# Grouped-query scores in pairs of heads, with the keys' low parts multiplied on 64 rows of TensorE

## The chip, the cores and the metric

The kernel runs on one core of a Trainium2 chip. The metric is the device time of one execution in microseconds (us). Three runs of the kernel before gave 1169.85, 1170.03 and 1171.18; the median is 1170.03.

## What is computed

Two layers of an encoder over 512 positions of width 1024, all in float32. Each layer projects the input into three groups of heads, mixes positions in each, projects back, adds and normalises, and then runs a gated FFN of width 2816. The change concerns the second group, grouped-query attention: 8 query heads of dimension 64 share 2 key/value heads.

```python
def gqa_attention(q, k, v):          # q: (b, s, 2, 4, 64), k and v: (b, s, 2, 64)
    scale = B_HEAD_DIM ** -0.5

    def block(qb):                   # 128 queries at a time
        s = jnp.einsum('bqhgd,bkhd->bhgqk', qb, k).astype(jnp.float32) * scale
        p = jax.nn.softmax(s, axis=-1).astype(v.dtype)
        return jnp.einsum('bhgqk,bkhd->bqhgd', p, v)

    return sweep_query_blocks(block, q)
```

## The kernel before

**Precision.** A float32 operand is kept as two parts of a faster matmul type, a high part (a rounded copy) and a low part (what the rounding left). A product is then high by high, high by low and low by high, three matmuls into one PSUM bank (`mm`, L240). Conversions are a copy on ACT and a subtraction on DVE or POOL (`put`, L248).

**Scores of the second group.** A head has only 64 dimensions, so the 128 rows of TensorE hold two parts at once. `qTB` (L176) has a slice of 128 rows by 512 queries for each of the 8 heads: for head (j, c), with j the key/value head and c = 0 to 3, the 64 rows of half j (`own`) hold the query's high part, the 64 rows of the other half its low part (L730 to L734). `kT` (L170) has two slices for each j: the key's high part on both halves (slice 2j), and its low part on both halves (slice 2j + 1; the second half is a copy by POOL, L717). One head is then two matmuls of 128 rows by 512 columns, first by slice 2j, then by slice 2j + 1 (L863, L864); they give all four products of parts.

**Softmax.** In `attn_b` (L837), for each block `qb` of 128 queries, each j and each c: the two score matmuls into one of three banks in turn (5, 6, 7; `score_banks`), the maximum (DVE, L866), its product with the head's scale (DVE, L869), the exponential with its sum (ACT, L873), the reciprocal (DVE, L875) and the normalisation (DVE, L876) into one of four slots of `E`. The head is put on a list (`pend`); as soon as three are on it, the oldest is finished (L841): four transposes on TensorE (L91) into one of two banks, and a copy to `W[j]` by ACT (L848). After the last head of a block, `pv_b` (L885) multiplies the probabilities with the values: 8 float32 matmuls whose results are 64 columns wide, j = 1 and j = 0 in turn on the two halves of TensorE's columns (the trace has two records for each).

**Order.** Each part of a layer is a generator; `Flow.run` (L105) advances the one of lowest rank whose time has come, by a planner's clock that each matmul advances by the cost written in its call (0.216 for the two score matmuls). A scheduler then moves the instructions of each engine by the priorities in `PRI` (L51) and by its own estimate of when operands are ready. While `attn_b` waits for softmax, `main` (L1089) fills TensorE with the query projection, then with `w_out` (L897): first the rows of the first and third group (`mixAC`), later those of this group (`mixB`), always three matmuls at a time. Each engine runs its instructions strictly in the order that comes out.

Of the kernel before, what the change touches and what calls it, by code (L numbers as in the profile page):

```python
# [14 lines left out]
AF = mybir.ActivationFunctionType  # L15
ALU = mybir.AluOpType
AX = mybir.AxisListType
PSUM = bass.MemoryType.PSUM

P = 128  # L20
# [9 lines left out]
LAT = {"c out": 1.6, "c": 1.05, "rope_a": 2.23, "split": 3.7, "turned": 0.61, "mix": 1.69, "rope_k": 4.08, "rope_q": 16.38, "split_k": 45.7, "soft_a": 2.05, "soft_b": 2.99, "copy": 1.27, "norm_a": 4.33, "put": 0.72, "ln": 4.93}  # L30
RATE = {"rank0": 3.09, "rank1": 2.96, "rank2": 0.16, "rank3": 4.47, "rank4": 4.88, "rank5": 32.35, "rankpv": 2.01, "rankev": 0, "rankx": 0, "a": 2.42, "a1": 2.34, "b": 0.12}
KNOBS = {"pin": 0, "pool1": 2, "pool2": 0, "pool3": 0, "poolac": 0, "poolbb": 1, "da": 2, "db": 3, "t2": 1, "rsb": 1, "ntail": 6, "qm": 1, "sb": 1, "cb": 0, "actdiv": 0, "kdup": 1, "splitq": 0, "splitk": 0, "ropet": 1, "aorder": 0}
# [14 lines left out]
def r(ap):  # L47
    return ap.bitcast(F32R)
# [223 lines left out]
def build(nc, tc, d, ctx_pools):  # L272
    pool, psum = ctx_pools
    k = Trunk(nc, tc, d, pool, psum)
    NS = 2
    X, xT, B, st, ident = k.X, k.xT, k.banks, k.st, k.ident
    ACT, DVE, POOL, SYNC = nc.scalar, nc.vector, nc.gpsimd, nc.sync
    F = PE = k.flow
# [4 lines left out]
    def small(n):  # L283

        if stp[0] + n > st.shape[1]:
            stp[0] = KEEP
        a = st[:, stp[0]:stp[0] + n]
        stp[0] += n
        return a
# [153 lines left out]
    def load_gb(l, which):  # L443
        SYNC.dma_start(out=k.GB[:, 0:D], in_=d[f"ln{which}_g"][l:l + 1, :].broadcast_to([P, D]))
        SYNC.dma_start(out=k.GB[:, D:2 * D], in_=d[f"ln{which}_b"][l:l + 1, :].broadcast_to([P, D]))
# [23 lines left out]
    def transposes(out, src):  # L469
        for c in range(4):  # L470
            PE.transpose(out[:, c * P:(c + 1) * P], src(c), ident)
# [6 lines left out]
    turn_banks, score_banks, prob_banks = (itertools.cycle(B[i] for i in b) for b in (tb_, ((5, 6, 7), (5, 6, 7, 2))[0], (3, 4)))  # L478

    def layer(l):  # L480
# [219 lines left out]
        def turn_b():  # L700
            yield ev("c mixed")
            kb = B[2]
            for tb in range(NT):
                yield ev("rope k", tb)
                PE.transpose(kb[:, tb * P:(tb + 1) * P], k.t1[tb % 2][:, 0:P], ident)
                busy.discard(tb % 2)

            with pri("kev"):
                for j in range(2):
                    own = slice(64 * j, 64 * j + 64)  # L710
                    other = slice(64 * (1 - j), 64 * (1 - j) + 64)
                    for u in (own, other):
                        ACT.copy(out=r(k.kT[u, 2 * j]), in_=kb[own])
                        if u is own or not KNOBS["kdup"]:
                            DVE.tensor_tensor(out=r(k.kT[u, 2 * j + 1]), in0=kb[own], in1=k.kT[own, 2 * j], op=ALU.subtract)
                    if KNOBS["kdup"] == 1:
                        POOL.tensor_copy(out=r(k.kT[other, 2 * j + 1]), in_=k.kT[own, 2 * j + 1])  # L717
                    elif KNOBS["kdup"] == 2:
                        ACT.copy(out=r(k.kT[other, 2 * j + 1]), in_=k.kT[own, 2 * j + 1])
            F.mark(ev("k"), 1.0)  # L720
            yield ev("scores a", 0)
            k.start_q_b(l)
            for tb in range(NT):
                yield ev("rope q", tb)
                with pri("qev"):
                    tbk = next(turn_banks)
                    transposes(tbk, lambda c: k.t1[tb % 2][:, c * P:(c + 1) * P])
                    busy.discard(tb % 2)
                    tv = tbk.rearrange("p (c t) -> p c t", c=4)
                    qv = k.qTB.rearrange("p (c j) t -> p c j t", j=2)[:, :, :, tb * P:(tb + 1) * P]  # L730
                    for j in range(2):
                        own, other = slice(64 * j, 64 * j + 64), slice(64 * (1 - j), 64 * (1 - j) + 64)
                        ACT.copy(out=r(qv[own, :, j]), in_=tv[own])
                        DVE.tensor_tensor(out=r(qv[other, :, j]), in0=tv[own], in1=qv[own, :, j], op=ALU.subtract)  # L734
                F.mark(ev("q", tb), LAT["turned"])
            k.start_mix_b(l)
            load_gb(l, 1)
            F.mark(ev("mix b"))


        def attn_a():
# [5 lines left out]
            for hp in range(2):  # L747
# [3 lines left out]
                for qb in range(NT):  # L751
                    for hh in range(2):
                        e = [E[:, (2 * (i % 2) + m) * T:(2 * (i % 2) + m + 1) * T] for m in range(2)]
                        i += 1
                        with pri("soft_a"):
                            ss = [s0v[:, qb, hh:hh + 1], small(1)]
                            for m in range(2):
                                S = next(score_banks)
                                PE.matmul(S, r(qk[0][:, 2 * hh + m, qb * P:(qb + 1) * P]), r(qk[1][:, 2 * hh + m]), 0.216, start=True, stop=True)
                                nm = small(1)  # L760
                                DVE.tensor_reduce(out=nm, in_=S, op=ALU.max, axis=AX.X, negate=True)
                                ACT.activation(out=e[m], in_=S, func=AF.Exp, bias=nm, accum_out=ss[m])
                            r1 = small(1)
# [73 lines left out]
        def attn_b():  # L837
            yield ev("pv a", 1)
            pend = []

            def finish(job):  # L841
                qb, j, c, p_, t = job
                yield max(0.0, t - F.now)
                with pri("turn_pb"):
                    tbk = next(prob_banks)
                    transposes(tbk, lambda c_: p_[:, c_ * P:(c_ + 1) * P])
                    wT = W[j].rearrange("p k (c q) -> p k c q", c=4)
                    ACT.copy(out=wT[:, :, c], in_=tbk.rearrange("p (k q) -> p k q", k=NT))  # L848
                if j == 1 and c == 3:
                    if qb == 0:  # L850
                        yield ev("mix b")
                    F.add(pv_b(qb), RATE['rankpv'])
                    yield ev("pv b", qb)

            n = 0
            for qb in range(NT):
                yield ev("q", qb)
                for j in range(2):
                    for c in range(4):
                        t_s = F.now  # L860
                        with pri("soft_b"):
                            S = next(score_banks)
                            for i in range(2):  # L863
                                PE.matmul(S, r(k.qTB[:, 2 * c + j, qb * P:(qb + 1) * P]), r(k.kT[:, 2 * j + i]), 0.216, start=i == 0, stop=i == 1)  # L864
                            nm = small(1)
                            DVE.tensor_reduce(out=nm, in_=S, op=ALU.max, axis=AX.X, negate=True)  # L866
                            sc = rsq[:, qb, 2 * c + j:2 * c + j + 1]
                            nb = small(1)
                            DVE.tensor_scalar_mul(out=nb, in0=nm, scalar1=sc)  # L869
                            p_ = E[:, (n % 4) * T:(n % 4 + 1) * T]  # L870
                            n += 1
                            s_ = small(1)
                            ACT.activation(out=p_, in_=S, func=AF.Exp, bias=nb, scale=sc, accum_out=s_)  # L873
                            rs = small(1)
                            DVE.reciprocal(out=rs, in_=s_)  # L875
                            DVE.tensor_scalar_mul(out=p_, in0=p_, scalar1=rs)  # L876
                        pend.append((qb, j, c, p_, F.now + LAT["soft_b"]))
                        yield RATE["b"] / 2
                        if len(pend) >= KNOBS['db']:
                            yield from finish(pend.pop(0))  # L880
                        yield max(0.0, t_s + RATE["b"] - F.now)
            for job in pend:
                yield from finish(job)

        def pv_b(qb):  # L885
            yield LAT["turned"]
            with pri("pv_b"):
                pv = B[2]
                for kb in range(NT):
                    for j in (1, 0):  # L890
                        PE.matmul(pv[64 * j:64 * j + 64, :], k.V[:, kb, 256 + j * 64:256 + (j + 1) * 64], W[j][:, kb], 0.44,
                                  start=kb == 0, stop=kb == NT - 1)
                k.put([m[:, :, qb * P:(qb + 1) * P] for m in k.mixB], pv.rearrange("p (c q) -> p c q", c=4))
            F.mark(ev("pv b", qb))
            F.mark(ev("mix b", qb), LAT["put"])
# [292 lines left out]
```

## Time and profile before

| | |
|---|---|
| median of three runs | 1170.03 us |
| the profiled execution's own time | 1170.78 us |
| its span | 1169.0 us |
| TensorE (PE) busy | 1145.8 us |
| DVE, ACT, POOL busy | 840.9, 624.9, 128.8 us |
| granted clock of TensorE | 0.996 of full speed over the span |

The span runs from the first to the last instruction; the execution's own time has 1.78 us around it. The busy time of TensorE counts a matmul until its modelled end, and matmuls are pipelined (one starts every 0.23 us, each lasts 0.40), so a share of 98% says that it hardly ever waits, not that it is at its peak. The second group's softmax stands twice in the span: from 123 to about 215 us in the first layer, and from 706 to about 798 us in the second.

### The profile page before, as it was taken

To read this page: it belongs to the slowest core of one execution; us is meant where nothing else is said; L and a number is where in the kernel's file an instruction comes from. 1 tells how busy PE (TensorE), PEld (TensorE's weight loads), DVE (VectorE), ACT (ScalarE), POOL (GpSimd) and SP (SyncE) were. 2 spreads that over 40 slices of the span, in tenths; PEclk is the share of its full clock that TensorE was granted. 3 is DMA by queue.
4 is the path that set the end of the run, shared out by engine and by line. 5 is a ranking of instruction groups with operands and counts; after the bars stand their busy time and mean duration, and the time that the engine had idled before them with its cause. 6 is when DMAs were issued, how large, how long until landed. Compare 5 with 4: busy or idle time off the path is not lost.

```text
span 1169.0 us, 18110 instructions
## 1 busy us (share of the span) xinstructions
PE 1145.8 (98%) x6930; PEld 977.8 (84%) x6930; DVE 840.9 (72%) x1532; ACT 624.9 (53%) x1348; POOL 128.8 (11%) x118
## 2 busy tenths in 40 slices
PE   9999899999999999999989998999999999999997
PEld 7787676799999999888768776767999999998886
DVE  5778977886888887333764889778777888873346
ACT  5778866454555555322254788654545655552220
POOL 1233230100000000000231342301000000000001
PEclk9999999999999999999999999999999999999999
DMA  8402140253242312334051021303432424132321
GB/s 286 151 1 91 37 127 1 91 163 108 73 135 83 115 68 81 100 91 126 25 152 62 2 89 45 119 1 107 146 108 73 145 73 133 49 91 90 96 85 73
DMA packets 32775, 107.86 MB, mean 92 GB/s; under 512 B 4657, under 2 KB 5681, under 8 KB 32689
## 3 DMA queue, kind: packets, MB, share of 16 engines
q1 hardware_dynamic: 32688, 106.71, 28.7%
q8 instruction: 54, 0.88, 0.3%
q14 instruction: 33, 0.26, 0.1%
HBM read 104.60 MB, written 2.10 MB: 91 GB/s over the span
## 4 chain that ended last, share of the span: by engine, by line
PE 87%; DVE 4%; DMA 3%; issue 3%; ACT 2%; POOL 2%; SPq 0%; POOLq 0%; ACTq 0%; DVEq 0%
PE bank L87 81%; PE bank L91 5%; DMA RAW<-w_in 2%; POOL st L292 1%; DVE XT L252 1%; ACT va L819 1%; DMA we<-w_in 1%; DVE st L866 0%; POOL rope L603 0%; POOL RING L266 0%; ACT RING L251 0%; DVE qTB L734 0%; DVE va L827 0%; DVE earlyr L252 0%; DVE RING L252 0%
## 5 line engine op out<-in xcount | busy, mean ns | idle before, releaser
L87 PE MATMUL bank<-XT,RING 128*128 128x256 f32 (+1 forms) x2304 | 305.6, 293 | 0.0
L87 PEld LDWEIGHTS bank<-XT,RING 128*128 128x128 f32 x2304 | 293.3, 191 | 7.7
L87 PE MATMUL bank<-RING,XT 128*128 128x512 f32 x576 | 160.8, 409 | 2.7 <-DVE RING L266 2.0
L292 POOL TENSOR_TENSOR st<-st 128x1 f32<-128x1 f32 (+2 forms) x44 | 54.1, 1229 | 929.1 <-DVE st L431 799.7
L251 ACT CAST RING<-ffnwe 128x512 fp32r<-128x512 f32 x156 | 96.0, 620 | 103.3 <-PE bank L87 61.5
L251 ACT CAST RING<-RAW 128x1024 fp32r<-128x1024 f32 (+1 forms) x114 | 97.0, 854 | 80.3 <-PE bank L87 33.4
L252 DVE TENSOR_TENSOR RING<-ffnwe,RING 128x512 fp32r<-128x512 f32 x156 | 107.1, 689 | 42.7 <-ACT RING L251 23.5
L87 PEld LDWEIGHTS bank<-RING,XT 128*128 128x128 f32 x576 | 106.7, 192 | 26.4 <-DVE RING L266 2.6
L252 DVE TENSOR_TENSOR RING<-RAW,RING 128x1024 fp32r<-128x1024 f32 (+1 forms) x106 | 101.8, 962 | 34.8 <-ACT RING L251 27.6
L87 PE MATMUL bank<-blkr,RING 128*128 128x256 f32 x864 | 105.5, 282 | 0.0
L87 PEld LDWEIGHTS bank<-blkr,RING 128*128 128x128 f32 x864 | 103.8, 189 | 0.0
L87 PE MATMUL bank<-RING 128*128 128x512 f32 x384 | 88.5, 390 | 0.0
L87 PEld LDWEIGHTS bank<-RING 128*128 128x128 f32 x384 | 72.0, 188 | 15.1
L91 PE MATMUL bank<-ident,we 128*128 128x128 f32 x400 | 62.0, 274 | 5.7 <-DVE va L827 5.5
L91 PEld LDWEIGHTS bank<-ident,we 128*128 128x128 f32 x400 | 47.9, 140 | 22.4 <-ACT rope L662 4.4
L873 ACT ACTIVATE we<-bank,st 128x512 f32<-128x512 f32 x64 | 50.5, 790 | 8.1 <-DVE st L869 7.7
L344 DVE TENSOR_TENSOR ffnwe<-ffnwe 128x512 f32<-128x512 f32 x80 | 54.6, 685 | 0.3
L87 PE MATMUL bank<-blkq,RING 128*128 128x256 f32 x432 | 54.3, 282 | 0.0
L87 PE MATMUL bank<-XT,mixAC 128*128 128x512 f32 x192 | 52.3, 404 | 0.6 <-DVE XT L252 0.5
L87 PEld LDWEIGHTS bank<-blkq,RING 128*128 128x128 f32 x432 | 52.6, 189 | 0.0
L848 ACT COPY we<-bank 128x512 f32<-128x512 f32 x64 | 37.8, 592 | 25.6 <-PE bank L91 25.6
L866 DVE TENSOR_REDUCE st<-bank 128x1 f32<-128x512 f32 x64 | 43.7, 686 | 10.7 <-PE bank L87 10.4
(210 smaller groups left out, 1925.9 us busy)
## 6 DMA issues: line engine op xcount, KB each, us to landing
RAW<-w_dn SPq DMA_DIRECT2D x44, 512.0 KB, 3.6
ffnwe<-w_gu SPq DMA_DIRECT2D x40, 512.0 KB, 4.5
RAW<-w_gu SPq DMA_DIRECT2D x32, 512.0 KB, 3.6
RAW<-w_in SPq DMA_DIRECT2D x28, 512.0 KB, 3.7
RAW<-w_out SPq DMA_DIRECT2D x16, 512.0 KB, 3.7
ffnw<-w_gu SPq DMA_DIRECT2D x16, 512.0 KB, 4.9
we<-xT SPq DMA_DIRECT2D x8, 256.0 KB, 5.4
X<-x SPq DMA_DIRECT2D x4, 512.0 KB, 5.4
```

The costliest lines, as they stand in the source:

```text
L87: self.pin(self.nc.tensor.matmul(out, lhs, rhs, **kw))
L91: self.pin(self.nc.tensor.transpose(out, src, ident))
L251: nc.scalar.copy(out=r(dst[0]), in_=src)
L252: (low or nc.vector).tensor_tensor(out=r(dst[1]), in0=src, in1=dst[0], op=ALU.subtract)
L292: POOL.tensor_tensor(out=out, in0=src, in1=k.mhalf[:, 0:n], op=ALU.pow)
L344: tc.keep_in_program_order(DVE.tensor_tensor(out=out, in0=x, in1=y, op=ALU.subtract))
L819: ACT.activation(out=oT[:, h * 64:(h + 1) * 64], in_=tbk[:, h * 64:(h + 1) * 64], func=AF.Square, accum_out=ms[:, h:h + 1])
L848: ACT.copy(out=wT[:, :, c], in_=tbk.rearrange("p (k q) -> p k q", k=NT))
L866: DVE.tensor_reduce(out=nm, in_=S, op=ALU.max, axis=AX.X, negate=True)
L873: ACT.activation(out=p_, in_=S, func=AF.Exp, bias=nb, scale=sc, accum_out=s_)
```

## The change

Two heads, (0, c) and (1, c), are taken together, with a bank each. For each, the first matmul stays as it was (128 rows by the key's high part, so high by high and low by high). The second now covers only the 64 rows of half j: the query's high part by the key's low part; low by low is dropped. The planner is told 0.108 for it, in place of 0.216. The two second matmuls stand on different halves of the rows. The copy of the low part to the other half of the rows (L717) is no longer made. Softmax of both heads follows, both go on the list, and as long as three or more are on it the oldest is finished.

```diff
                     for u in (own, other):
                         ACT.copy(out=r(k.kT[u, 2 * j]), in_=kb[own])
-                        if u is own or not KNOBS["kdup"]:
-                            DVE.tensor_tensor(out=r(k.kT[u, 2 * j + 1]), in0=kb[own], in1=k.kT[own, 2 * j], op=ALU.subtract)
-                    if KNOBS["kdup"] == 1:
-                        POOL.tensor_copy(out=r(k.kT[other, 2 * j + 1]), in_=k.kT[own, 2 * j + 1])
...
+                    DVE.tensor_tensor(out=r(k.kT[own, 2 * j + 1]), in0=kb[own], in1=k.kT[own, 2 * j], op=ALU.subtract)
...
             for qb in range(NT):
                 yield ev("q", qb)
-                for j in range(2):
-                    for c in range(4):
-                        t_s = F.now
-                        with pri("soft_b"):
-                            S = next(score_banks)
-                            for i in range(2):
-                                PE.matmul(S, r(k.qTB[:, 2 * c + j, qb * P:(qb + 1) * P]), r(k.kT[:, 2 * j + i]), 0.216, start=i == 0, stop=i == 1)
+                for c in range(4):
+                    t_s = F.now
+                    with pri("soft_b"):
+                        S = [next(score_banks) for _ in range(2)]
+                        q = [k.qTB[:, 2 * c + j, qb * P:(qb + 1) * P] for j in range(2)]
+                        for j in range(2):
+                            PE.matmul(S[j], r(q[j]), r(k.kT[:, 2 * j]), 0.216, start=True, stop=False)
+                        for j in range(2):
+                            own = slice(64 * j, 64 * j + 64)
+                            PE.matmul(S[j], r(q[j][own]), r(k.kT[own, 2 * j + 1]), 0.108, start=False, stop=True)
+                        for j in range(2):
                             nm = small(1)
...
-                        pend.append((qb, j, c, p_, F.now + LAT["soft_b"]))
-                        yield RATE["b"] / 2
-                        if len(pend) >= KNOBS['db']:
-                            yield from finish(pend.pop(0))
-                        yield max(0.0, t_s + RATE["b"] - F.now)
+                            pend.append((qb, j, c, p_, F.now + LAT["soft_b"]))
+                    yield RATE["b"] / 2
+                    while len(pend) >= KNOBS['db']:
+                        yield from finish(pend.pop(0))
+                    yield max(0.0, t_s + RATE["b"] - F.now)
```

The scheduler does not keep the four matmuls of a pair together. On TensorE, in the first layer before the change, the heads of a late block of queries stand like this (banks 74, 75 and 76 hold scores, 72 and 73 transposes):

```order
L87 MATMUL bank_74<-kT_518,qTB_858 128x512 x2
L87 MATMUL bank_70<-XT,mixAC_517 128x512 x3
L91 MATMUL bank_72<-ident,we_90 128x128 x4
L87 MATMUL bank_75<-kT_518,qTB_858 128x512 x2
L87 MATMUL bank_70<-XT,mixAC_517 128x512 x3
L91 MATMUL bank_73<-ident,we_90 128x128 x4
```

Each head has its two matmuls side by side, then three of `w_out`, then the four transposes of an earlier head. After the change, the same stretch of TensorE has this for one pair (of the two rows of a bank, the first is the matmul of 128 rows, the second that of 64):

```order
L87 MATMUL bank_74<-kT_518,qTB_856 128x512
L91 MATMUL bank_72<-ident,we_90 128x128
L87 MATMUL bank_75<-kT_518,qTB_856 128x512
L91 MATMUL bank_72<-ident,we_90 128x128
L87 MATMUL bank_74<-kT_518,qTB_856 128x512
L91 MATMUL bank_72<-ident,we_90 128x128
L87 MATMUL bank_75<-kT_518,qTB_856 128x512
L91 MATMUL bank_72<-ident,we_90 128x128
L91 MATMUL bank_73<-ident,we_90 128x128 x4
L87 MATMUL bank_69<-RING,mixBr1a_1387 128x512 x2
L87 MATMUL bank_69<-RING,mixBr1b_1388 128x512
```

The transposes have moved between the matmuls, and the two of 64 rows no longer follow each other. A pair whose matmuls do stay together stands, on TensorE in the same block, right ahead of the product with the values (bank 71):

```order
L87 MATMUL bank_76<-kT_518,qTB_856 128x512
L87 MATMUL bank_74<-kT_518,qTB_856 128x512
L87 MATMUL bank_76<-kT_518,qTB_856 128x512
L87 MATMUL bank_74<-kT_518,qTB_856 128x512
L87 MATMUL bank_71<-we_90,va_519 64x512 x8
```

In each layer 5 of the 16 pairs keep their two matmuls of 64 rows side by side (3 of them ahead of the product with the values, 2 ahead of transposes); in the other 11 something stands between, which makes 22 matmuls of 64 rows on their own, 17 followed by a transpose and 5 by a matmul of 128 rows.

## Rows read from the trace of the kernel before

**Rows 1.** The page's first part: span and busy time of each engine.
```profile
span 1169.0 us, 18110 instructions
PE 1145.8 (98%) x6930; PEld 977.8 (84%) x6930; DVE 840.9 (72%) x1532; ACT 624.9 (53%) x1348; POOL 128.8 (11%) x118
```

**Rows 2.** The page's fourth part: shares of the chain that ended last, by engine.
```profile
PE 87%; DVE 4%; DMA 3%; issue 3%; ACT 2%; POOL 2%; SPq 0%; POOLq 0%; ACTq 0%; DVEq 0%
```

**Rows 3.** Stretch, length; busy us (count): PE, PEld, DVE, ACT, POOL; clock; DMA, GB/s.
```profile
123.00:152.00 29.00, 25.63 (x137) 17.47 (x134) 26.39 (x64) 24.14 (x79) 7.42 (x5) 1.00 0.24 73
152.00:168.00 16.00, 15.94 (x70) 10.13 (x69) 10.21 (x20) 8.26 (x14) 9.71 (x4) 1.00 0.44 133
168.00:215.00 47.00, 47.00 (x252) 34.62 (x250) 38.18 (x100) 30.87 (x67) 1.56 (x2) 1.00 0.04 12
706.00:735.00 29.00, 25.55 (x134) 17.07 (x132) 26.54 (x65) 24.19 (x74) 7.41 (x5) 1.00 0.24 73
```

**Rows 4.** The chain that ended last, 123 to 152 us: start, us, what.
```profile
131.86 1.76 ACT va L819 x16
...
147.08 0.68 DVE qTB L734
```

**Rows 5.** TensorE's timeline, 171.3 to 174.6 us: start, us, engine, line, operation, count.
```profile
171.34 0.71 PE L87 MATMUL bank<-kT,qTB 128*128 128x512 f32 x2
171.88 0.86 PE L87 MATMUL bank<-XT,mixAC 128*128 128x512 f32 x3
172.59 0.60 PE L91 MATMUL bank<-ident,we 128*128 128x128 f32 x4
172.94 0.71 PE L87 MATMUL bank<-kT,qTB 128*128 128x512 f32 x2
```

**Rows 6.** TensorE's timeline in short windows around one product with the values.
```profile
153.24 0.40 PE L87 MATMUL bank<-XT,mixAC 128*128 128x512 f32 x1
153.56 0.65 PE L87 MATMUL bank<-we,va 128*64 128x512 f32 x2
...
154.90 0.60 PE L87 MATMUL bank<-we,va 128*64 128x512 f32 x2
155.43 0.96 PE L87 MATMUL bank<-XT,mixAC 128*128 128x512 f32 x3
```

**Rows 7.** The weight loads (PEld) of the same product with the values.
```profile
153.56 0.20 PEld L87 LDWEIGHTS bank<-we,va 128*64 128x64 f32 x4 [0.36 <-ACT we L848]
154.04 0.14 PEld L87 LDWEIGHTS bank<-we,va 128*64 128x64 f32 x2 [0.29 <-issue]
154.47 0.14 PEld L87 LDWEIGHTS bank<-we,va 128*64 128x64 f32 x2 [0.28 <-issue]
```

**Rows 8.** TensorE's timeline, 125.7 to 126.5 us: transposes whose weights were not loaded ahead.
```profile
125.75 0.63 PE L91 MATMUL bank<-ident,rope 128*128 128x128 f32 x4
```

**Rows 9.** Groups by line: count, busy us, mean ns of one, idle time before.
```profile
L866 DVE TENSOR_REDUCE st<-bank 128x1 f32<-128x512 f32 x64 | 43.7, 686 | 10.7 <-PE bank L87 10.4
L869 DVE TENSOR_SCALAR st<-st 128x1 f32<-128x1 f32 x64 | 13.1, 205 | 0.8
L873 ACT ACTIVATE we<-bank,st 128x512 f32<-128x512 f32 x64 | 50.5, 790 | 8.1 <-DVE st L869 7.7
L873 ACT ACTIVATION_READ_ACCUMULATOR we<-bank,st 128x1 f32 x64 | 13.1, 205 | 0.0
L875 DVE RECIPROCAL st<-st 128x1 f32<-128x1 f32 x64 | 10.1, 159 | 6.3 <-ACT we L873 5.6
L876 DVE TENSOR_SCALAR we<-we,st 128x512 f32<-128x512 f32 x64 | 34.1, 532 | 0.8
L717 POOL CAST kT<-kT 64x512 fp32r<-64x512 f32 x4 | 4.5, 1130 | 5.6 <-DVE kT L715 5.6
```

**Rows 10.** The same view: weight loads of the score matmuls and of the product with the values.
```profile
L87 PEld LDWEIGHTS bank<-kT,qTB 128*128 128x128 f32 x128 | 20.3, 190 | 9.1 <-ACT we L873 4.6 <-issue 3.2
L87 PEld LDWEIGHTS bank<-we,va 128*64 128x64 f32 x192 | 12.5, 136 | 24.1 <-issue 21.2 <-ACT we L848 2.2 <-ACT kT L713 0.7
```

More of the change, by code (lines that the diff above doesn't have):

```diff
@@ L713, in turn_b @@
                         ACT.copy(out=r(k.kT[u, 2 * j]), in_=kb[own])
-                        if u is own or not KNOBS["kdup"]:
-                            DVE.tensor_tensor(out=r(k.kT[u, 2 * j + 1]), in0=kb[own], in1=k.kT[own, 2 * j], op=ALU.subtract)
-                    if KNOBS["kdup"] == 1:
-                        POOL.tensor_copy(out=r(k.kT[other, 2 * j + 1]), in_=k.kT[own, 2 * j + 1])
-                    elif KNOBS["kdup"] == 2:
-                        ACT.copy(out=r(k.kT[other, 2 * j + 1]), in_=k.kT[own, 2 * j + 1])
+                    DVE.tensor_tensor(out=r(k.kT[own, 2 * j + 1]), in0=kb[own], in1=k.kT[own, 2 * j], op=ALU.subtract)
             F.mark(ev("k"), 1.0)
@@ L857, in attn_b @@
                 yield ev("q", qb)
-                for j in range(2):
-                    for c in range(4):
-                        t_s = F.now
-                        with pri("soft_b"):
-                            S = next(score_banks)
-                            for i in range(2):
-                                PE.matmul(S, r(k.qTB[:, 2 * c + j, qb * P:(qb + 1) * P]), r(k.kT[:, 2 * j + i]), 0.216, start=i == 0, stop=i == 1)
+                for c in range(4):
[9 more added lines that the diff above has]
+                        for j in range(2):
                             nm = small(1)
-                            DVE.tensor_reduce(out=nm, in_=S, op=ALU.max, axis=AX.X, negate=True)
+                            DVE.tensor_reduce(out=nm, in_=S[j], op=ALU.max, axis=AX.X, negate=True)
                             sc = rsq[:, qb, 2 * c + j:2 * c + j + 1]
@@ L872, in attn_b @@
                             s_ = small(1)
-                            ACT.activation(out=p_, in_=S, func=AF.Exp, bias=nb, scale=sc, accum_out=s_)
+                            ACT.activation(out=p_, in_=S[j], func=AF.Exp, bias=nb, scale=sc, accum_out=s_)
                             rs = small(1)
```

## The prediction

> **What bounds the kernel now.** I read the page first, then the stretches in which the change lies, then single instructions. TensorE is busy for 1145.8 of 1169.0 us [rows 1], and 87% of the chain that ended last lies on it, mostly from matmul to matmul [rows 2]. So a microsecond put on TensorE is a microsecond of time, wherever TensorE has no gap that could hold it. The table of stretches says where gaps are. From 123 to 152 us, where the first block of queries runs, TensorE is idle for 29.00 − 25.63 = 3.4 us and DVE is busy for 26.39; the chain runs there through ACT and DVE [rows 3, 4]. From 168 to 215 us, where blocks two to four run, TensorE is busy for all 47.00 us, at full clock [rows 3]. The second layer looks the same (706 to 735: 25.55 of 29.00) [rows 3]. In the dense stretch a head returns every 172.94 − 171.34 = 1.60 us: two score matmuls, three of `w_out`, four transposes, with no gap [rows 5]. That is the rhythm the change enters.
>
> **What is saved.** Three matmuls of 512 columns last 0.86 us and one 0.40, so one more costs (0.86 − 0.40) / 2 = 0.23 [rows 5, 6]. Where the two matmuls of 64 rows stand side by side, they use different halves of the rows and may run at once. The nearest thing in the trace, two matmuls on different halves of the columns, does so: the two records of a pair together last 0.65 at the start and 0.60 later, not twice that, and a pair follows a pair after 0.43 [rows 6, 7]. So such a pair saves 0.23. But the order has only 5 pairs a layer side by side, 10 of 32. The other 44 matmuls of 64 rows save nothing: each streams 512 columns by itself. The whole gain is 10 × 0.23 = 2.3 us.
>
> **What each visit to 64 rows costs.** The trace of before has no matmul on part of the rows; the nearest rows are those on part of the columns, and there changing over is not free. The step from the last full matmul to the first of 64 columns is 153.56 − 153.24 = 0.32, 0.09 over the usual 0.23 [rows 6]. The first pair takes 154.04 − 153.56 = 0.48, the next 0.43: 0.05 more, since its weights were not loaded ahead; the weight loads stand idle for 0.36 us before it [rows 7]. From the last pair back to a full matmul it is 155.43 − 154.90 = 0.53, 0.10 over 0.43; and the three full ones that follow last 0.96, not 0.86 [rows 5, 6]. Together 0.09 + 0.05 + 0.10 + 0.10 = 0.34 us a round trip. If a transpose follows, the last 0.10 shrinks to 0.03, for four transposes whose weights were not there take 0.63 against 0.60 [rows 5, 8]: 0.27. If the product with the values follows, its own way in and out was paid before, and 0.09 + 0.05 = 0.14 remains.
>
> The bounds: nothing, if rows need no change-over. Above, the weights of a score matmul load for 190 ns against 136 for 64 columns [rows 10], so 0.05 more on each of 54 visits, 2.7 us in all. I take the columns' price, the only measured change of the array's shape.
>
> The Trainium skill, "TensorEngine Tiling (Array Packing)", section Key Properties, states that changing the tiling mode, not just the tile, drains TensorE; rows and columns are both modes there. The trace agrees for columns (the 0.34 above); no run so far shows it for rows.
>
> **The sum on TensorE**, per layer: 17 single visits that end in a transpose, 17 × 0.27 = 4.6; 5 that end in a full matmul, 5 × 0.34 = 1.7; 2 pairs before transposes, 2 × (0.27 − 0.23) = 0.1; 3 pairs before the product with the values, 3 × (0.14 − 0.23) = −0.3. That is 6.1, and 12.2 for two layers. Of it one pair and four single visits per layer fall into the stretch with 3.4 us of idle time, 4 × 0.34 + 0.04 = 1.4. Some of these precede what the chain there waits for, some stand in a gap; I count half, which takes off 1.4 for both layers. **+10.8 us.**
>
> **What is late next.** A head's chain after its scores is maximum 0.69, scale 0.20, exponential 0.79 + 0.20, reciprocal 0.16, normalisation 0.53, or 2.6 us without hand-offs [rows 9]. Before, a head's transposes came after the scores of the next two heads, at least two rhythms of 1.60 = 3.2 us later, and nothing waited. Now the transposes of a pair stand inside the next pair, and its second head has to let the first one's exponential by (0.99), 3.6 us after its scores. Where only three matmuls of `w_out` stand between two pairs, TensorE has four transposes (0.44), three matmuls (0.69) and one score matmul (0.23) to do, 1.4 us after the last score and about 2 after the first: some 0.7 short. I find two such places in each of the six later blocks (three a layer): 12 × 0.7 = 8.4 us if every one binds, nothing if the time of the visits fills them. I take half: **+4.2 us**. ACT and DVE get no more work; in the dense stretch they are busy 30.87 and 38.18 of 47.00 [rows 3], so neither becomes the bound. The third score bank is tighter too (a pair's second head takes the bank of the last pair's first), but that exponential is done before the normalisation of the same head, so it binds no earlier.
>
> **What costs nothing.** The four POOL copies of the keys' low parts (1.13 us each) go [rows 9]; POOL is busy for 128.8 of 1169.0 us [rows 1], so this saves nothing on the path. No DMA is added, removed or moved past another queue.
>
> **Sum.** 1170.8 + 10.8 + 4.2 = 1185.8 us against the profiled execution's own time, which is 0.7 above the median of the runs: **1185 us** on their scale.
>
> **Rivals.**
> - *Rows change over freely* (faster). If weights for 64 rows load behind a matmul of 128 rows, as full weights do now, every visit is free and the pairs save 2.3 us: 1167.7. If besides a matmul of half the rows streamed in about half the time, as the planner's 0.108 has it, 64 × 0.115 = 7.4 us would go: 1162.7. It decides as soon as a visit costs less than about 2.3 / 54 = 0.04 us and the waits stay hidden. Against it stand the 0.34 of the columns and that no row shows a shorter stream. The Trainium skill, "TensorE: Matmul & The Clock Gate", Part 3, has row tiles start about 4 ns apart and run together; by its rule the 10 adjacent pairs alone would give these 2.3 us. The trace shows columns starting together, but with the price of getting there. Chance 0.12; waits of some microseconds would leave half of these cases at no change.
> - *The softmax chain sets the pace* (slower still). If in blocks two to four every pair waits for the last one's normalisation, a pair takes its chain of 2.6 plus the second maximum ahead of it on DVE (0.69), plus the 1.2 to 1.5 of its own remaining matmuls, about 4.6, against 3.2 for two heads before. Over 12 pairs a layer that is up to 24 × 1.4 = 34 us, less the `w_out` matmuls that then find room in it; with half of it 1170 + 17 + 10.8 = 1198. For it: the order on ACT and DVE puts both heads' exponentials and maxima side by side. Against: six `w_out` matmuls stand between most pairs. Chance 0.16.
> - *The visits are hidden.* If they cost half the columns' price, or the stretch with idle time swallows all of its share, and waits and visits fill the same time, 4 to 8 us remain: 1174 to 1178. Chance 0.10. Nothing but the stretch up to 152 us speaks for it.
>
> **How the numbers follow.** The forecast, columns' price with part of the waits, has 0.62 and reaches from 1170 + 8 = 1178 (few waits) to 1170 + 12.2 + 2.7 + 8.4 = 1193. The range takes in most of the two slower rivals: 1173 to 1199; below it lies the free change-over, above it the full pace of the chain. A difference of 0.2% (2.3 us) is about what a measurement tells from none. Faster by more than that needs the free visit and no waits, 0.06; within it, 0.07; slower 0.87.
>
> **What would show it.** In the changed profile: a step of about 0.32 instead of 0.23 from a full matmul to one of 64 rows, and weight loads idle before it; adjacent 64-row matmuls starting together; the dense stretch of each layer longer by 5 to 9 us at the same clock; waits of TensorE's transposes for L877, 0 to 8 us in all. The forecast is wrong if 64-row weights load during the matmul before them, or if waits for the normalisation exceed the visits' cost.

## The result and the profile after

The changed kernel takes 1190.49 us (median of four runs, 1190.08 to 1191.23); the kernel before took 1169.94 beside it. The ratio is 1.0175 [1.0157, 1.0193]: 20.5 us slower. The profiled run took 1190.41 us, and its span is 19.6 us longer than that of [rows 1].

The page's first part, the clock row of its second part and the shares of its chain:

```profile
span 1188.6 us, 18111 instructions
PE 1163.9 (98%) x6930; PEld 977.8 (82%) x6930; DVE 841.6 (71%) x1532; ACT 623.1 (52%) x1348; POOL 123.5 (10%) x114
...
PEclk9999899999999999999999999999999999999999
...
PE 85%; ACT 3%; DVE 3%; issue 2%; POOL 2%; DMA 1%; POOLq 0%; ACTq 0%; DVEq 0%
```

The score matmuls in the groups by line and shape (columns as [rows 9]):

```profile
L87 PE MATMUL bank<-kT,qTB 64*128 64x512 f32 x64 | 27.1, 501 | 0.0
L87 PE MATMUL bank<-kT,qTB 128*128 128x512 f32 x64 | 25.4, 444 | 2.6 <-ACT we L874 2.6
```

Against [rows 1], the count of TensorE's instructions is the same and its busy time is 18.1 us longer; the loads, DVE and ACT hardly moved. A matmul on 64 rows lasts no less than one on 128. So the time is on TensorE, and two stretches are to be told apart. Same columns as [rows 3]:

```profile
123.00:152.00 29.00, 25.70 (x110) 15.73 (x109) 24.22 (x59) 21.40 (x78) 7.47 (x5) 0.88 0.25 67
142.30:149.10 6.80, 5.45 (x18) 3.90 (x18) 5.44 (x11) 2.92 (x6) 1.98 (x2) 0.50 0.15 25
152.00:168.00 16.00, 16.00 (x80) 12.71 (x78) 9.07 (x18) 9.95 (x18) 8.70 (x4) 1.00 0.41 117
168.00:222.00 54.00, 53.97 (x257) 33.16 (x255) 40.05 (x103) 31.27 (x70) 2.44 (x2) 1.00 0.06 19
706.00:735.00 29.00, 26.33 (x125) 16.52 (x123) 24.29 (x62) 25.16 (x97) 9.06 (x6) 1.00 0.13 37
736.20:739.60 3.40, 3.40 (x15) 2.71 (x13) 3.33 (x6) 1.85 (x5) 0.85 (x1) 0.50 0.00 0
```

The dense stretch is still full, at full clock, as foreseen. The first stretch is new: 110 matmuls and transposes stand in the 29 us that held 137 [rows 3], and for 6.80 us of it the granted clock is 0.50, the lower of its two levels (1.2 in place of 2.4 GHz). [Rows 3] have 1.00 there.

TensorE's waits over the whole span of the changed kernel (what it waited for: us in all, times, longest), four rows of the view:

```profile
PE bank L87 <- DVE rope L669: 4.1, 2, 2.0
PE bank L87 <- ACT we L874: 2.6, 2, 1.3
PE bank L91 <- DVE va L822: 2.3, 2, 1.2
...
PE bank L91 <- DVE we L877: 0.6, 2, 0.3
```

The wait that the forecast named, transposes for the normalisation in L877, comes to 0.6 us in two layers. In its place stand two waits a layer in the first stretch, 2.0 and 1.3 us (the first two rows).

### The profile page after: what moved, and what is told of

It is laid out like the page before. It is cut to its first block, busy times and chain, and to the rows that moved or that the text cites. A ratio compares the mean times of both kernels' runs of the same rounds, so it can differ in the third digit from the quotient of the medians.

```text
span 1188.6 us, 18111 instructions
## 1 busy us (share of the span) xinstructions
PE 1163.9 (98%) x6930; PEld 977.8 (82%) x6930; DVE 841.6 (71%) x1532; ACT 623.1 (52%) x1348; POOL 123.5 (10%) x114
## 4 chain that ended last, share of the span: by engine, by line
PE 85%; ACT 3%; DVE 3%; issue 2%; POOL 2%; DMA 1%; POOLq 0%; ACTq 0%; DVEq 0%
PE bank L87 79%; PE bank L91 6%; POOL st L292 2%; DMA RAW<-w_in 1%; ACT va L814 1%; ACT we L874 1%; DVE X L437 0%; DVE st L867 0%; ACT rope L662 0%; POOL RING L266 0%; ACT RING L251 0%; DVE st L425 0%; ACT XT L251 0%; POOL rope L603 0%; DVE rope L669 0%
## 5 line engine op out<-in xcount | busy, mean ns | idle before, releaser
L91 PE MATMUL bank<-ident,we 128*128 128x128 f32 x400 | 69.7, 284 | 2.9 <-DVE va L822 2.3
L87 PE MATMUL bank<-kT,qTB 128*128 128x512 f32 (+1 forms) x128 | 51.0, 472 | 2.6 <-ACT we L874 2.6
```

The source lines that it names most:

```text
L87: self.pin(self.nc.tensor.matmul(out, lhs, rhs, **kw))
L91: self.pin(self.nc.tensor.transpose(out, src, ident))
```

## What the runs had to tell apart

The theory after the result was the forecast's: visits to 64 rows cost about 11 us, the rest is the pairing of heads. The rival was that the order of the program, whatever the rows, costs more. The kernels were run in three groups of four, each group beside runs of the kernel before on its own chip (medians 1169.48, 1170.18 and 1170.23).

### First group: rows, order and adjacency

**e_single** is the kernel before, every engine's order unchanged; only the second score matmul of each head is put on 64 rows, 64 visits in all.

```diff
+                                rows = slice(64 * j, 64 * j + 64) if i else slice(0, P)
-                                PE.matmul(S, r(k.qTB[:, 2 * c + j, qb * P:(qb + 1) * P]), r(k.kT[:, 2 * j + i]), 0.216, start=i == 0, stop=i == 1)
+                                PE.matmul(S, r(k.qTB[rows, 2 * c + j, qb * P:(qb + 1) * P]), r(k.kT[rows, 2 * j + i]), 0.216, start=i == 0, stop=i == 1)
```

> The kernel before, each engine's order unchanged, with one edit: the second score matmul of each head runs on its own 64 rows instead of 128. All 64 matmuls of 64 rows then stand alone among full ones, nothing runs beside them. Theory (each visit to 64 rows costs about 0.34 us between full matmuls): 64 x 0.34 = 22 us, about half of the 8 in each first block hidden, so 1189 to 1194 us. Rival (visits are cheap, the change's loss comes from taking heads in pairs and the order that follows): no change, 1169 to 1172.

Measured: 1188.03 us, ratio 1.0159 [1.0144, 1.0175], 18.6 us slower than before. TensorE's timeline in its dense stretch:

```profile
186.00 0.93 PE L87 MATMUL bank<-kT,qTB 128*128 128x512 f32 x2
186.85 0.96 PE L87 MATMUL bank<-XT,mixAC 128*128 128x512 f32 x3
187.65 0.60 PE L91 MATMUL bank<-ident,we 128*128 128x128 f32 x4
188.01 0.91 PE L87 MATMUL bank<-kT,qTB 128*128 128x512 f32 x2
```

Against [rows 5] the two score matmuls last 0.93 instead of 0.71, the three after them 0.96 instead of 0.86, and a head returns after 2.01 instead of 1.60 us: a visit between matmuls of 128 rows costs about 0.40. 64 × 0.40 would be 25.6; 18.6 came, a little under the 1189 expected. Since the order is that of the kernel before, the same matmul can be found in both traces (the profiled runs differ by 16.8 us). In the first layer the first 12 of the 32 visits, before 153.6 us, put TensorE back by 2.0 us instead of 4.8: they fill time in which TensorE waited before [rows 3]. The other 20 put it back by 7.1, or 0.35 each. The second layer is the same, and 1.0 us is made up between the layers.

**e_full** is the changed kernel with the second matmuls back on 128 rows (and POOL's copies with them); the order on TensorE, DVE, ACT and SP is that of the changed kernel.

```diff
                     DVE.tensor_tensor(out=r(k.kT[own, 2 * j + 1]), in0=kb[own], in1=k.kT[own, 2 * j], op=ALU.subtract)
+                    POOL.tensor_copy(out=r(k.kT[other, 2 * j + 1]), in_=k.kT[own, 2 * j + 1])
...
-                            PE.matmul(S[j], r(q[j][own]), r(k.kT[own, 2 * j + 1]), 0.108, start=False, stop=True)
+                            PE.matmul(S[j], r(q[j]), r(k.kT[:, 2 * j + 1]), 0.108, start=False, stop=True)
```

> The changed kernel with the second matmuls of a pair back on 128 rows, and the POOL copy back that this needs; TensorE, DVE, ACT and SP run exactly the order of the changed kernel. Theory: without visits, and without the 2.3 us that adjacent pairs save, only the order's own cost is left: 1170 to 1175 us, the dense stretch back to its old rhythm, and waits for the normalisation between 0 and 4 us. Rival (order): it stays at 1185 or above. On the half clock of the changed profile at 142 and 736 us: if the order's wait at 139 to 143 us brings it, it is here too; if the visits bring it, it is gone.

Measured: 1178.68 us, 1.0079 [1.0064, 1.0094]: 9.2 us slower than before without one visit. That missed the theory's 1170 to 1175 and the rival's 1185 or above. The change splits into 9.2 us of order and 20.5 − 9.2 = 11.3 us of visits, and the 9.2 had no cause yet.

**e_adj** holds the two 64-row matmuls of every pair together, 32 visits in place of 54.

```diff
+                        tc.cur_priority -= 2000
...
-                            PE.matmul(S[j], r(q[j][own]), r(k.kT[own, 2 * j + 1]), 0.108, start=False, stop=True)
+                            tc.keep_in_program_order(nc.tensor.matmul(S[j], r(q[j][own]), r(k.kT[own, 2 * j + 1]), start=False, stop=True))
+                            F.now += 0.108
+                        tc.cur_priority += 2000
```

> The changed kernel with the two matmuls of 64 rows held together in all 32 pairs (raised priority, and the order of the program kept for them). Theory: 32 visits in place of 54, each saves 0.23 by running two at once and costs 0.27 to 0.35: 32 x (0.04 to 0.12) = 1 to 4 us, plus 0 to 4 us of the order: 1171 to 1178. Rival (order sets the pace): 1185 or above. If row changes were free: 1163 to 1168.

Measured: 1187.34 us, 1.0152 [1.0137, 1.0167], 17.9 us slower: far above the theory's 1171 to 1178, and where the rival (the order sets the pace) put it. Adjacency did not remove what the order costs. What it does to a pair shows beside the next kernel.

**e_adj_same** is e_adj with both 64-row matmuls on rows 0 to 63, so that the second head's high part by the key's low part is left out.

```diff
-                            tc.keep_in_program_order(nc.tensor.matmul(S[j], r(q[j][own]), r(k.kT[own, 2 * j + 1]), start=False, stop=True))
+                            tc.keep_in_program_order(nc.tensor.matmul(S[j], r(q[j][0:64]), r(k.kT[0:64, 1]), start=False, stop=True))
```

> As the kernel with all pairs adjacent, but both matmuls of 64 rows use rows 0 to 63 (for the second head this takes the wrong parts, so its low-part term is left out of the result), so that they cannot run at once. Theory: the saving of 0.23 a pair goes, 32 x 0.23 = 7.4 us more than the kernel with the pairs on different halves. Rival (different halves do not run at once either): the same time as that kernel.

Measured: 1192.32 us, 1.0194 [1.0177, 1.0211], 5.0 us over e_adj (7.4 expected). A pair on TensorE's timeline, of e_adj and then of e_adj_same:

```profile
178.13 0.49 PE L865 MATMUL bank<-kT,qTB 64*128 64x512 f32 x2
```

```profile
186.18 0.73 PE L865 MATMUL bank<-kT,qTB 64*128 64x512 f32 x2
```

On different halves of the rows two matmuls take 0.49 us together, no longer than one alone; on the same half 0.73. So they do run at once, and in the trace that is worth 0.24 a pair, the 0.23 that the forecast gave. In time it is 5.0 us over 32 pairs, 0.16 a pair: in the first layer none of it shows before 151.5 us. The Trainium skill, "TensorE: Matmul & The Clock Gate", Part 3, has row tiles start about 4 ns apart; in the records of e_adj the second matmul of a pair starts 3 to 4 ns after the first, which agrees.

### Second group: is it the pairing in the first block?

The new theory for the 9.2 us was that pairs disturb the first block, the one with idle time, and nothing later. Four kernels have the changed way of writing the keys; the first three take block one head by head, as before.

```diff
                 yield ev("q", qb)
+                if qb == 0:
+                    for j in range(2):
+                        for c in range(4):
...
+                    continue
```

**e_full_late** has blocks two to four in pairs on 128 rows.

> The first block of 128 queries of each layer as before (heads one by one), blocks two to four in pairs in the changed way, all matmuls on 128 rows: no visit to 64 rows, and pairs only where TensorE was dense. Theory (the order's loss of about 9 us lies in the first block, where waits and a half clock appeared): 1168 to 1173 us, no half clock near 142 and 730 us. Rival (taking heads in pairs loses in the dense blocks, by the longer softmax chain): 1176 or above.

Measured: 1182.28 us, 1.0102 [1.0087, 1.0117], 12.1 us slower. The theory fell: with the first block taken head by head, the loss is no smaller. It is in the place that the theory named (1st to 17th score 24.3 us, 17.8 before; half clock from 143.1 and 730.2 us), but pairs there are not its cause. The number is one that the rival allowed (1176 or above); e_full_ko below decides against the rival.

**e_pair_late** is the same with blocks two to four on 64 rows (42 visits, 6 of them by two matmuls).

> The same kernel, the same order on every engine, with the second matmuls of blocks two to four on 64 rows: 42 visits, 36 of them single and 6 adjacent pairs. Theory: nothing hides them there, so 36 x (0.35 to 0.40) + 6 x (0.40 - 0.23) = 14 to 15.5 us over the kernel on 128 rows in this order, 1183 to 1188 us. Rival (visits were dear only in the stretch with waits): under 7 us over it.

Measured: 1193.83 us, 1.0202 [1.0185, 1.0219]: the base was wrong again, but the difference of 11.6 us to e_full_late is the price of 36 single visits and 6 double ones, less than the 14 to 15.5 expected.

**e_adj_late** has the held pairs of e_adj in blocks two to four.

> First block as before, blocks two to four in pairs whose two matmuls of 64 rows are held together: 24 visits with two matmuls each. Theory: 24 x (0.40 - 0.23) = 4 us over the kernel before, or 1172 to 1176. Rival: that all-adjacent pairs lost 18 us by the visits themselves: 24 of 32 of it, 1183 or above.

Measured: 1181.49 us, 1.0093 [1.0078, 1.0108]. Missed by the same base; beside e_full_late the held visits cost nothing that can be told (−0.8 us, though in another order).

**e_adj_full** is e_adj's order on 128 rows throughout.

> The order of the kernel with all pairs adjacent, with every matmul on 128 rows. Theory: the visits made up 32 x (0.40 - 0.23) = 5.4 us of its 17.9 at most, the rest is its order in the first block, so 1182 to 1186. Rival (the visits made up most of it): 1170 to 1176.

Measured: 1182.99 us, 1.0111 [1.0096, 1.0126]: the time expected, though e_full_late had just refuted the reason given for it. The order on TensorE is that of e_adj. That ran in the first group and is 17.9 us over the runs of before beside it; this one is 12.8 over its own. The difference of 5.0 us is 32 held visits at 0.16 net. So even a visit that two matmuls share costs more than the matmul that it saves.

### Third group: the keys

All kernels with a loss of order had one line in common that the forecast had passed over. Before, the low part of the keys is subtracted right after the first high copy (ACT, DVE, ACT, then POOL); the change has the subtraction behind both copies (ACT, ACT, DVE).

**e_kev** is the kernel before with that alone: heads singly, all matmuls on 128 rows, POOL's copies kept.

```diff
                     for u in (own, other):
                         ACT.copy(out=r(k.kT[u, 2 * j]), in_=kb[own])
-                        if u is own or not KNOBS["kdup"]:
-                            DVE.tensor_tensor(out=r(k.kT[u, 2 * j + 1]), in0=kb[own], in1=k.kT[own, 2 * j], op=ALU.subtract)
...
+                    DVE.tensor_tensor(out=r(k.kT[own, 2 * j + 1]), in0=kb[own], in1=k.kT[own, 2 * j], op=ALU.subtract)
+                    POOL.tensor_copy(out=r(k.kT[other, 2 * j + 1]), in_=k.kT[own, 2 * j + 1])
```

> The kernel before with one edit, in the writing of the keys alone: for each j both ACT copies of the high part come first, then the DVE subtraction of the low part, then the POOL copy, as in the changed kernel (where that copy is gone); before, the subtraction stood between the two ACT copies. Heads one by one, all matmuls on 128 rows. What is computed and the number of instructions are the same, but in the order that comes out the projection matmuls that stood after the first group's last product with the values stand ahead of it. Theory: this alone is the order's loss (waits and half clock in the first block): 1178 to 1183 us, with the half clock near 143 and 730. Rival (the pairs make the loss): 1169 to 1172.

Measured: 1177.8 us, 1.0062 [1.0048, 1.0076]: 7.6 us slower, 0.2 us short of the theory's range. Each engine has as many instructions of work as before; the scheduler has put TensorE's in another order. TensorE's timeline of e_kev:

```profile
128.72 1.86 PE L87 MATMUL bank<-RING,XT 128*128 128x512 f32 x7
...
131.56 3.65 PE L87 MATMUL bank<-we,va 128*64 128x512 f32 x16
...
137.53 0.86 PE L87 MATMUL bank<-XT,mixAC 128*128 128x512 f32 x3
140.37 0.74 PE L87 MATMUL bank<-kT,qTB 128*128 128x512 f32 x2 [1.98 <-ACT we L869]
140.94 1.46 PE L87 MATMUL bank<-XT,mixAC 128*128 128x512 f32 x3
144.37 1.12 PE L91 MATMUL bank<-ident,we 128*128 128x128 f32 x4 [1.96 <-DVE va L823]
```

and of the kernel before, where the sixteen matmuls of that product (`we`, `va`: the last of the first group of heads) begin at 126.31:

```profile
126.31 3.65 PE L87 MATMUL bank<-we,va 128*64 128x512 f32 x16
...
130.46 0.86 PE L87 MATMUL bank<-RING,XT 128*128 128x512 f32 x3
...
132.50 1.56 PE L87 MATMUL bank<-RING,XT 128*128 128x512 f32 x6
133.90 0.62 PE L87 MATMUL bank<-kT,qTB 128*128 128x512 f32 x2
134.36 0.85 PE L87 MATMUL bank<-RING,XT 128*128 128x512 f32 x3
137.01 0.63 PE L91 MATMUL bank<-ident,we 128*128 128x128 f32 x4 [1.80 <-DVE va L827]
```

The projections (`RING`, `XT`) wait for nothing here, so the kernel before uses twelve of them as filler while the product's result goes through its normalisation on ACT, POOL and DVE (that chain began at 131.86 [rows 4]). In e_kev they stand ahead of the product, which comes 131.56 − 126.31 = 5.3 us later; too little is left to fill with, and TensorE waits 1.98 us for a score bank that an exponential still reads (L869) and 1.96 us for the normalised product (L823). The clock falls after the first of the two; in the second layer (waits of 1.99 and 2.51 us) it falls within the second. In the changed kernel the same product comes at 132.08, and the waits of 1.3 and 2.0 us follow. The stretches of e_kev:

```profile
123.00:152.00 29.00, 25.02 (x121) 17.24 (x120) 25.52 (x62) 22.76 (x83) 7.44 (x5) 0.88 0.29 90
141.10:147.90 6.80, 4.84 (x18) 3.46 (x17) 5.39 (x8) 2.26 (x6) 2.19 (x2) 0.50 0.18 48
706.00:735.00 29.00, 24.50 (x111) 17.02 (x111) 26.28 (x63) 22.17 (x83) 7.44 (x5) 0.88 0.23 72
728.20:735.00 6.80, 5.95 (x21) 4.80 (x22) 6.08 (x13) 3.28 (x7) 0.00 (x0) 0.50 0.50 151
```

Busy time at half clock counts double (one transpose follows another after 0.21 us there, after 0.11 at full clock): (4.84 + 5.95) / 2 = 5.4 us lost. Idle time against [rows 3]: (25.63 − 25.02) + (25.55 − 24.50) = 1.7 us more. Together 7.1 of the 7.6 us.

**e_full_ko** has pairs everywhere on 128 rows, with the keys written as before.

```diff
-                            PE.matmul(S[j], r(q[j][own]), r(k.kT[own, 2 * j + 1]), 0.108, start=False, stop=True)
+                            PE.matmul(S[j], r(q[j]), r(k.kT[:, 2 * j + 1]), 0.108, start=False, stop=True)
```

(against the changed kernel, whose four lines on the keys are put back as well).

> Pairs as in the changed kernel, all matmuls on 128 rows, and the keys written as in the kernel before. Theory: the order's loss is gone: 1168 to 1173 us, no half clock near 143 and 730. Rival (the pairs make the loss): 1176 to 1181.

Measured: 1170.6 us, 1.0001 [0.9992, 1.001]. **With the keys written as before, taking heads in pairs costs nothing.** TensorE's waits from 123 to 160 us; the 1.80 for `va` in the kernel before is down to 0.9:

```profile
PE bank L91 <- DVE va L827: 0.9, 1, 0.9
PE bank L87 <- ACT we L879: 0.3, 1, 0.3
```

**e_kevold** is the changed kernel with only the keys written as before: the order of e_full_ko, with 52 single visits and 6 by two matmuls.

```diff
-                    DVE.tensor_tensor(out=r(k.kT[own, 2 * j + 1]), in0=kb[own], in1=k.kT[own, 2 * j], op=ALU.subtract)
+                        if u is own or not KNOBS["kdup"]:
+                            DVE.tensor_tensor(out=r(k.kT[u, 2 * j + 1]), in0=kb[own], in1=k.kT[own, 2 * j], op=ALU.subtract)
+                    if KNOBS["kdup"] == 1:
+                        POOL.tensor_copy(out=r(k.kT[other, 2 * j + 1]), in_=k.kT[own, 2 * j + 1])
```

> The changed kernel, pairs and 64 rows, with the keys written as in the kernel before (with the POOL copy, which nothing reads). The same order as the kernel with pairs on 128 rows of this call. 58 visits, 52 single and 6 adjacent pairs. Theory: only the visits are left: over the kernel with pairs on 128 rows by 52 x (0.35 to 0.40) + 6 x 0.17 = 19 to 22 us less 3 to 8 in the first blocks, so 1182 to 1190. Rival (visits are mostly hidden once the order is right): under 1178.

Measured: 1182.57 us, 1.0105 [1.0091, 1.0119]: 12.0 us over e_full_ko, all of it the visits. Its first stretch is at full clock:

```profile
123.00:152.00 29.00, 28.44 (x133) 17.21 (x132) 25.02 (x65) 24.81 (x82) 7.59 (x5) 1.00 0.19 58
```

**e_adj_late_ko** puts the pieces together as well as they go: keys as before, block one head by head, the 24 later pairs held together on 64 rows (the edits of e_kevold, e_full_late and e_adj at once).

> Keys written as in the kernel before; first block head by head; blocks two to four in pairs whose two matmuls of 64 rows are held together: 24 visits of two matmuls. Theory: 24 x (0.40 - 0.23) = 4 us over the kernel before: 1172 to 1175. Rival (pairs run together pay for the visit): 1166 to 1169. It is the best that this change can be by the prices measured so far, and by them still slower than before.

Measured: 1173.32 us, 1.0026 [1.0017, 1.0036], as expected: 3.1 us slower than before, 24 × 0.13. No form that was run beats the kernel before.

The same split by landmarks, from TensorE's timeline in the first layer (start of the 1st, 17th and 64th record of a score matmul, us; 16 belong to a block):

| kernel | keys | visits | 1st | 17th | 64th | 1st to 17th | 17th to 64th |
|---|---|---|---|---|---|---|---|
| before | old | 0 | 123.08 | 140.84 | 206.20 | 17.8 | 65.4 |
| e_full_ko | old | 0 | 122.94 | 139.98 | 202.93 | 17.0 | 63.0 |
| e_single | old | 64 | 122.66 | 142.49 | 214.60 | 19.8 | 72.1 |
| e_kevold | old | 58 | 123.47 | 141.52 | 209.33 | 18.1 | 67.8 |
| e_kev | new | 0 | 124.65 | 148.49 | 210.18 | 23.8 | 61.7 |
| e_full | new | 0 | 124.94 | 147.40 | 207.93 | 22.5 | 60.5 |
| after | new | 54 | 124.37 | 147.59 | 213.88 | 23.2 | 66.3 |

New keys lengthen the way to the 17th score by 5 to 6 us, and 1.5 to 3.7 come back behind it. Visits show on both sides of the 17th. After less e_full is 0.8 us ahead of it (4 single and 2 double visits) and 5.8 behind it; e_kevold less e_full_ko is 1.0 (6 single, 1 double) and 4.9; e_single less before is 2.1 (8 single) and 6.8 (24 single).

## Why the prediction was right, and where it was not

Slower was forecast with 0.87, at 1185 us in 1173 to 1199; 1190.49 came. The direction and the larger of the two terms were right; the smaller term was wrong, and one that belonged in the sum was missing. That the time still lies well inside the range is in part luck: the room above was kept for a softmax chain that binds everywhere (8.4 us), and a line of the keys that the forecast passed over cost about as much (9.2).

- **What bounds the kernel: right.** The added time is on TensorE, and the dense stretch stayed full at clock 1.00.
- **What a pair side by side saves: right.** 0.23 was read from the rhythm; 0.24 came in the trace between e_adj and e_adj_same. That such a visit still loses, 0.27 − 0.23 = 0.04, was right in sign; held pairs cost 0.13 to 0.16 net.
- **The visits, +10.8: right, by two errors that nearly cancel.** They cost 11.3 us in the changed order and 12.0 in that of e_kevold. The price of the columns carried over to the rows, a little low. TensorE's timeline of the changed kernel shows both changes of a pair whose transposes have moved in between:

```profile
173.07 0.27 PE L91 MATMUL bank<-ident,we 128*128 128x128 f32 x1
173.27 0.50 PE L87 MATMUL bank<-kT,qTB 64*128 64x512 f32 x1
173.70 0.33 PE L91 MATMUL bank<-ident,we 128*128 128x128 f32 x1
173.96 0.50 PE L87 MATMUL bank<-kT,qTB 64*128 64x512 f32 x1
174.39 0.33 PE L91 MATMUL bank<-ident,we 128*128 128x128 f32 x1
```

  and e_full, where the same instructions stand in the same order on 128 rows:

```profile
171.91 0.27 PE L91 MATMUL bank<-ident,we 128*128 128x128 f32 x1
171.94 0.48 PE L87 MATMUL bank<-kT,qTB 128*128 128x512 f32 x1
172.25 0.27 PE L91 MATMUL bank<-ident,we 128*128 128x128 f32 x1
172.28 0.48 PE L87 MATMUL bank<-kT,qTB 128*128 128x512 f32 x1
172.60 0.27 PE L91 MATMUL bank<-ident,we 128*128 128x128 f32 x1
```

  From a transpose to the score matmul it is 0.20 and 0.26 in place of 0.03, from there to the next transpose 0.43 in place of 0.32. The whole takes 1.32 instead of 0.69 us, and the last transpose 0.06 longer: 0.32 to 0.35 for a visit among transposes, against 0.27 forecast. Between full matmuls it is 0.40, against 0.34 (0.39 with its upper bound). So the prices were 0.05 to 0.08 low. With them the 44 single visits alone would come to 34 × (0.32 to 0.35) + 10 × 0.40 = 14.9 to 15.9 us, an estimate, and 11.3 came for all 54; the 10 double ones add next to nothing (beside e_full, 0.11 each ahead of transposes, −0.03 ahead of the product with the values). So some 4 us did not show in the time, in place of the 1.4 that the forecast took off for waits. In e_single what does not show lies mostly up to 153.6 us, where TensorE waits.
- **The loads before a visit: right.** The weight loads around one pair of the changed kernel, with the idle time that the forecast named:

```profile
167.68 0.19 PEld L87 LDWEIGHTS bank<-kT,qTB 64*128 64x128 f32 x2 [0.36 <-issue]
168.11 0.20 PEld L87 LDWEIGHTS bank<-we,va 128*64 128x64 f32 x4 [0.25 <-issue]
```

  The 0.36 us before the 64-row load is as long as what [rows 7] show before the first 64 columns; in e_full the load at this place has no idle time before it. The Trainium skill, "TensorEngine Tiling (Array Packing)", section Key Properties, said that a change of mode drains TensorE; e_single shows a price for rows too, 0.40 us for the way in and out, but not whether it is a drain.
- **"What is late next", +4.2: wrong.** The softmax chain of a pair was to hold up the transposes. It held them up for 0.6 us in all, and e_full_ko, with every pair, is at 1.0001. The working counted the filler at its tightest places only, two in each later block, took some 0.7 us to be short there, and counted half. The places are tight but not short, and it is the order that sees to it, not the time of the visits: e_full_ko has no visit, and its transposes wait for the normalisation at one place a layer, for 0.3 us. The second rival, that this chain sets the pace, fell with it.
- **"What costs nothing": wrong by omission.** It dealt with POOL's copies, rightly, and with no other line of the keys. The subtraction that moved behind both ACT copies is in the diff. By itself it is worth 7.6 us (e_kev), with heads in pairs 9.2 (e_full); pairs alone cost nothing (e_full_ko). This term takes the place of the 4.2 and makes the sum 11.3 + 9.2 = 20.5. In other orders on 128 rows the new keys cost 12.1 (e_full_late) and 12.8 (e_adj_full); what makes these differ was not looked into.
- **The rivals.** Rows do not change over freely: e_single. The visits are not hidden: up to 153.6 us a bit more than half of their price is, in e_single, and hardly any of it later.
- **The signs named.** The step from a full matmul to one of 64 rows is 0.33 us ahead of the product with the values (0.32 forecast), and adjacent ones start together. The dense stretch, from the 17th to the 64th score, is only 0.9 us longer than before, not 5 to 9: pairs shorten it by 2.4 (e_full_ko) and the new keys by 2.4 more (e_full), before the visits lengthen it by 5.8.

That the lower clock is the larger part of the keys' term is worked out from rows (5.4 of 7.6 us), not tested by itself: no kernel had these waits without the lower clock. The changed kernel and all eight others with the new way of writing keys have a stretch at 0.50 that begins between 141 and 145 us, and one that begins between 727 and 738; the kernel before and the four others with the old way have neither (another stretch at 0.50, near 590 to 601 us, comes in kernels of both kinds, the kernel before among them). Why the scheduler moves the projections when one subtraction is written two places later (it goes by estimates and priorities) was not followed up.

## What to carry to other kernels

A matmul on part of the rows between matmuls on all of them cost TensorE some 0.32 to 0.40 us here, and it streamed no faster (0.50 us by the profile, 0.44 on 128 rows); two that ran at once saved one matmul of 0.23, which was not enough to pay for the visit. Price each visit by its neighbours in the scheduled order, not by the source, and separate it from the order by running the same order on full tiles. A line that moves in a diff counts, even if the engine's work stays the same: look in the order of the engine that bounds the kernel for work without waits (filler) that has moved out of a stretch that needs it.

## What the runs showed of the hardware that was not expected

In a kernel that is otherwise dense, waits of a few microseconds were dear: in e_kev TensorE waits 1.98 us until 140.37, the granted clock is 0.50 from 141.10 on for 6.80 us, and the second wait of 1.96 lies within that. The lower clock cost more (5.4 us in two layers) than the added idle time (1.7). The kernel before waits 1.80 us until 137.01 and keeps 1.00 over the whole stretch [rows 3]; what of the activity around tells the two apart is not settled. And which way of a visit is dear depends on its neighbours. Between full matmuls (e_single beside the kernel before, medians from 154 to 216 us) the way in takes 0.41 in place of 0.31, the way out 0.43 in place of 0.23, and the matmul behind it still 0.10 more; among transposes the way in is the dearer one (0.17 to 0.23 more, against 0.11).
